# Summing the mLSTM half of y on GpSimd while heads are stored, in a decoder layer on one core

## The chip, the cores and the metric

One Trainium2 chip, one of its cores. The metric is the device time of one execution in microseconds (us). The engines go by the names of the profile: PE is TensorE, PEld its weight loads, DVE is VectorE, ACT is ScalarE, POOL is GpSimd, and SP is SyncE, which here only issues DMAs.

## The reference, cut to what matters

One layer of a decoder trunk, 1024 tokens, width 2048, all in float32:

```python
proj = x @ w_in                      # columns split over two head groups
# group A: sparse attention, 8 heads of 128 columns
score = sum_h w_i[h] * relu(q_i[h] @ k_i.T); sel = top_k(score, 256)
y_a = (softmax(q_lat @ c_sel.T + bias) @ c_sel @ w_uv) * silu(z_a)       # (1024, 1024)
# group B: mLSTM, 4 heads of 256 columns, chunkwise, then per-head norm
y_m = norm(h_m) * mh_norm_g * sigmoid(o_m) * silu(z_m)                   # (1024, 1024)
y = concat([y_a, y_m]) @ w_out
x = layer_norm(ALPHA * x + y)
```

## The kernel before

Work is laid out with 128 partitions (`P`), time in two halves `top` (tokens 0 to 511) and `bot` (512 to 1023). Every product that has to be exact to float32 is made of three passes over a rounded high part and a low rest: `split` casts on ACT (L106) and subtracts on DVE (L107). The order of instructions on each engine is set at compile time by a scheduler that follows priorities, edges written by hand (`issue_after`, `after`, `add_manual_dep`) and a model of time; at run time each engine takes its instructions in that order.

The stages, in order:

1. Projection of x for the indexer and search of the top 256 keys, then first halves of the other projections (to about 946 us).
2. The mLSTM stage: `Unit`s finish the other projections on PE (L679, 7 products of 12 matmuls each; sums of weights on POOL at L663, one low part on POOL at L668, accumulating weight DMAs on POOL at L644), and between them the four mLSTM heads run (`mlstm(h)`). Head h-1 is stored inside `mlstm(h)`, after the convolutions that give q and k: `stores(h-1)` calls `mlstm_store` for the two 128-column blocks j of the head, which transposes the head's output on PE, multiplies by the gate tile `sg` on DVE and writes `sg` (128 x 1024) to `y_d[8 + 2h + j]` in DRAM (L919). The last head is stored at the end of the stage.
3. Attention, 8 heads of 4 query blocks. `weights` adds the mask and bias tile on POOL (`nm`, L1249), reduces logits on DVE (L1256), and scales the exponentials by 1/sum on POOL (query tiles 4 to 7) or DVE (L1264). `turn` transposes them on PE (L1281), `mix` multiplies by the values (L1293 to L1296). A head's result goes to `y_d[h]`.
4. The output product with w_out, in blocks of Strassen-Winograd form: `Product(p, c)`, where p = 0 is the mLSTM half of y (`y_d[8..15]`) and p = 1 the attention half (`y_d[0..7]`). Each half has four blocks a11, a12, a21, a22 (columns j = 0 or 1, `top` or `bot`), each of 4 tiles of 128 x 512. The form also needs sums of these blocks, with signs already put in at storing: s1 = a21 + a22, s2 = s1 + a11, s4 = s2 + a12, s3 = a11 + a21.

The sums are prepared in DRAM while attention runs. `y_steps` names, by query block (4h + n), which steps are issued: a plain DMA on SP from DRAM to DRAM (L1154), or a DMA on POOL that adds to DRAM (`accum_op=OP.add`, L1151). Each step is two DMAs of 512 KB. So attention issues 10 copies on SP and 10 accumulating DMAs on POOL: s1, s2, s4 and s3 of p = 0, and s3 of p = 1. On POOL they stand between `nm` and the scaling of `weights`. `y_form` then loads the kept sums at the output (L1182). Sums that are not kept are loaded block by block (L1185) and added by POOL DMAs into SBUF (L1188).

SBUF working tiles of 128 x 1024 float32 come from one tag, `s4`, with 11 buffers; in the mLSTM stage q, k, the head's two outputs, `sg`, `ri`, `pq`, `kw`, `pqh`, `pql`, `kws`, `vraw`, `vh`, `vl` all live there. Raw weights have 6 buffers (`wraw`), split weights 4 pairs.

Of the kernel before, what the change touches and what calls it, by code (L numbers as in the profile page):

```python
# [15 lines left out]
OP = mybir.AluOpType  # L16
# [3 lines left out]
P = 128  # L20
# [46 lines left out]
SUMS = ("s1", "s2", "s3", "s4")  # L67
# [33 lines left out]
def kernel(ctx, tc, a, out):  # L101
    nc = tc.nc
    vec, act, pool, pe, sync = nc.vector, nc.scalar, nc.gpsimd, nc.tensor, nc.sync
# [36 lines left out]
    def small(j, p=P):  # L140
# [5 lines left out]
    y_d = dp.tile([KT, P, T], F32, name="y_d")  # L146
# [2 lines left out]
    part_d = dp.tile([NU, P, 2, T], F32, name="part_d")  # L149
    z_d = dp.tile([8, P, 2, 512], F32, name="z_d")  # L150
    y_form_d = {n: dp.tile([P, 4, 512], F32, name=f"y_form_d{n[0]}{n[1]}")
                for n in ((0, "s1"), (0, "s2"), (0, "s4"), (0, "s3"), (1, "s3"))}
    if_d = dp.tile([2 * H_M, T], F32, name="if_d")
    rows_d = dp.tile([H_M, 2, T], F32, name="rows_d")
    decay_d = dp.tile([H_M, NCH], F32, name="decay_d")
# [10 lines left out]
    def s4(name, shape=(P, T), dt=F32):  # L166
        return sp.tile(list(shape), dt, name=name, tag="s4", bufs=S4)
# [30 lines left out]
    def bank(name, shape=(P, 512)):  # L198
        return ss.tile(list(shape), F32, name=name, tag="b")
# [112 lines left out]
    n = len(marks)  # L312
# [261 lines left out]
    for i in range(2):  # L574
        ps = bank("vb")[0:H_A, 0:NV // 2]
        s = slice(i * NV // 2, (i + 1) * NV // 2)
# [23 lines left out]
    top, bot = halves  # L600
# [238 lines left out]
    for j in range(8):  # L839
        n = len(marks)  # L840
# [67 lines left out]
    def y_sign(left, upper):  # L908

        return -1.0 if left == upper else 1.0  # L910

    def mlstm_store(h, j, hs, sg):
        for half in range(2):
            ps = bank("ht")
            for c in range(4):
                pe.transpose(ps[:, c * P:(c + 1) * P], hs[half][:, c, j * P:(j + 1) * P], ident)
            vec.scalar_tensor_tensor(out=sg[:, halves[half]], in0=ps, scalar=y_sign(h < 2, half == 0),
                                     in1=sg[:, halves[half]], op0=OP.mult, op1=OP.mult)
        sync.dma_start(y_d[8 + 2 * h + j], sg)  # L919

    def mlstm_half(h, half, n, q, k):

        s = halves[half]
        ri = s4("ri", (P, 2, 512))
        sync.dma_start(ri, bcast_rows(rows_d[h, :, s]))
        pool.affine_select(out=ri[:, 0].rearrange("p (c l) -> p c l", l=L),
                           in_=ri[:, 0].rearrange("p (c l) -> p c l", l=L),
                           compare_op=OP.is_ge, fill=BIG, base=0,
                           pattern=[[0, 4], [1, L]], channel_multiplier=-1)
        pq = s4("pq", (P, 2, 512))  # L930
        for c in range(4):
            cs = slice(c * L, (c + 1) * L)
            act.activation(pq[:, 0, cs], ri[:, 0, cs], AF.Exp, scale=-1.0,
                           bias=gcol[:, half * 4 + c, 0, h:h + 1])
        with after(n):
            pt = bank("ktp")
            for c in range(4):
                cs = slice((half * 4 + c) * L, (half * 4 + c + 1) * L)
                pe.transpose(pt[:, c * P:(c + 1) * P], k[:, cs], ident)
            ps = bank("s")  # L940
            for c in range(4):
                cs = slice((half * 4 + c) * L, (half * 4 + c + 1) * L)
                pe.matmul(ps[:, c * L:(c + 1) * L], k[:, cs], q[:, cs], start=True, stop=True)
        kw = s4("kw", (P, 4, DK))
        vec.tensor_tensor(kw, pt.rearrange("p (c d) -> p c d", d=DK),
                          gcol[:, half * 4:half * 4 + 4, 1, h:h + 1].broadcast_to([P, 4, DK]),
                          op=OP.mult)
        vec.tensor_tensor(pq[:, 0], ps, pq[:, 0], op=OP.mult)
        vec.tensor_tensor(pq[:, 1], q[:, s], ri[:, 1], op=OP.mult)
        pqh, pql = s4("pqh", (P, 2, 512), F32R), s4("pql", (P, 2, 512), F32R)  # L950
        split(pqh, pql, pq)
        kws = s4("kws", (P, 2, 4, DK), F32R)
        split(kws[:, 0], kws[:, 1], kw)
        return pqh, pql, kws
# [139 lines left out]
    n = len(marks)  # L1094
# [14 lines left out]
    op = ctx.enter_context(tc.tile_pool(name="op", bufs=1))  # L1109
    Y = {}  # L1110

    def y_rows(p, name):

        j, s = {"a11": (0, top), "a12": (1, top), "a21": (0, bot), "a22": (1, bot)}[name]
        return [y_d[8 * (1 - p) + 4 * j + k][:, s] for k in range(4)]

    def y_tiles(pool_, name, tags=(None, None)):

        f = []
        for c, t in zip("hl", tags):  # L1120
            if pool_ is sp:
                y = [s4(f"y{name}{c}", (P, 2, 512), F32R) for _ in range(2)]
                f.append([y[k // 2][:, k % 2] for k in range(4)])
            else:
                y = pool_.tile([P, 4, 512], F32R, name=f"y{name}{c}", tag=t or f"y{name}{c}", bufs=1)
                f.append([y[:, k] for k in range(4)])
        return f
# [8 lines left out]

    chain, last_sum = [None], [None]

    def y_half(p, name, u):

        j, s = {"a11": (0, top), "a12": (1, top), "a21": (0, bot), "a22": (1, bot)}[name]
        k0 = 8 * (1 - p) + 4 * j + 2 * u
        return y_d[k0:k0 + 2, :, s].rearrange("k p c -> p k c")

    def y_step(p, name, src, more):

        for u in range(2):
            dst = y_form_d[p, name][:, 2 * u:2 * u + 2]
            if more:
                with tc.issue_after(last_sum[0].ins):  # L1150
                    pool.dma_start(dst, y_half(p, src, u), accum_op=OP.add)  # L1151
            else:
                src_ = y_form_d[p, src][:, 2 * u:2 * u + 2] if src in SUMS else y_half(p, src, u)
                d = sync.dma_start(dst, src_)  # L1154
                tc.add_manual_dep(d.ins, last_sum[0].ins.name, mybir.DependencyInfo(
                    mybir.DependencyClass.NoSync, mybir.DependencyReason.DATA), reason="pace")

    y_steps = {6: ((0, "s1", "a21", False), (0, "s3", "a11", False)),
# [4 lines left out]

    def y_form(p, name, pool_):

        early = p == 0 and name == "s1"
        kept = (p, name) in y_form_d
        if name in ("s2", "s4") and p:
            raw = chain[0]
        elif early:  # L1170
            raw = [s4("yraw", (P, 2, 512)) for _ in range(2)]
            raw = [raw[k // 2][:, k % 2] for k in range(4)]
        else:
            raw = oq.tile([P, 4, 512], F32, name="u" if name in ("s1", "s2", "s3") and (p == 0 or name == "s1") else "t")
            raw = [raw[:, k] for k in range(4)]
        if name == "s1":
            chain[0] = raw
        load, more = {"s1": ("a21", "a22"), "s2": (None, "a11"), "s4": (None, "a12")}.get(name, (name, None))
        f = y_tiles(sp if early else pool_, name)
        for k in range(4):  # L1180
            if kept:
                sync.dma_start(raw[k], y_form_d[p, name][:, k])  # L1182
            else:
                if load:
                    sync.dma_start(raw[k], y_rows(p, load)[k])  # L1185
                if more:
                    with tc.issue_after(last_sum[0].ins):
                        pool.dma_start(raw[k], y_rows(p, more)[k], accum_op=OP.add)  # L1188
            split(f[0][k], f[1][k], raw[k])
        return f  # L1190

    with ExitStack() as ph:
# [126 lines left out]
        for h in range(H_A):  # L1319
            qk = k_next + q_next  # L1320
            gt, tb = head_inputs(h) if h else head_0
            if h == 0:
                sync.dma_start(gt, gate_a[0])
            if h + 1 < H_A:
                k_next, q_next = keys(h + 1), queries(h + 1)
            order = range(4) if h < H_A - 1 else range(3, -1, -1)
            for n, p in enumerate(order):
                pr = weights(p, qk, tb)
                for step in y_steps.get(4 * h + n, ()):
                    y_step(*step)  # L1330
                consume(AHEAD - 1)
                if n == 0 and h % 2 == 0:
                    while blocks:
                        mix(blocks.pop(0))
                    values_of[h // 2] = values(h // 2)
                units.append((h, p, pr, gt, n == 3))
# [212 lines left out]
    for t in range(8):  # L1549
# [5 lines left out]
        for n in range(2):  # L1555
            ps = bank("zps") if t % 2 else lps()
            for kt in range(8):
                f = Y[("a11", "a12", "a21", "a22")[2 * i + kt // 4]]
# [57 lines left out]
```

## Time and profile before

| | |
|---|---|
| median of 3 runs | 1867.68 us (1867.62 to 1868.41) |
| profiled execution, own time | 1868.55 us |
| its span, first to last instruction | 1866.7 us |
| PE busy | 97% of the span |
| DVE, ACT, POOL busy | 71%, 50%, 20% |
| mean granted TensorE clock | 0.992 of full speed |

A row of a windows view gives the busy time of each engine inside a stretch: PE idle is the length of the stretch less PE busy. The granted clock is in its own column; at a clock below 1.00 the same matmuls take longer, so length x (1 - clock) is time lost too.

### The profile page before, as it was taken

Reading aid. Unit: us, or ns where it says so; the run is one execution under the profiler, and the core shown is the slowest. Engines: PE = TensorE matmul, PEld = TensorE weight load, DVE = VectorE, ACT = ScalarE, POOL = GpSimd, SP = SyncE. Lnnn points to the kernel's source line nnn. Section 1 sums busy time; section 2 is a strip of 40 time slices with the busy share of each in tenths; the row PEclk is TensorE's granted clock in tenths of the full one; section 3 lists DMA queues with packets and bytes.
Section 4 is the critical chain, followed back from the end, with each engine's and each line's share of the span. In section 5 each row is a group of like instructions: output and inputs, shape, how many; then the busy total and the mean of one; then the engine's idle time right before and its main releaser. Section 6 shows DMA issues by size and latency. Waiting matters only on the chain. (4 is left out here: it accounts for less than half of the span.)

```text
span 1866.7 us, 25500 instructions
## 1 busy us (share of the span) xinstructions
PE 1804.7 (97%) x8740; PEld 1518.4 (81%) x8740; DVE 1334.5 (71%) x2464; ACT 935.3 (50%) x1712; POOL 379.1 (20%) x368
## 2 busy tenths in 40 slices
PE   8999999999999999999999999989989999999997
PEld 7987888888877788788888787868878998788885
DVE  6264665887788778655667677777889876576788
ACT  5334444666658633432455565565655665343421
POOL 0021221011001000011322222222455541011132
PEclk9999999999999999999999999999999999999998
DMA  7355335346546557766565646556686437874764
GB/s 271 81 167 197 121 100 149 107 122 178 137 120 173 136 144 235 208 197 196 154 202 154 169 142 188 138 164 186 211 221 149 139 103 226 260 200 118 191 182 143
DMA packets 140699, 311.75 MB, mean 167 GB/s; under 512 B 14936, under 2 KB 25944, under 8 KB 134680
## 3 DMA queue, kind: packets, MB, share of 16 engines
q1 hardware_dynamic: 119416, 269.21, 44.4%
q0 software_dynamic: 21152, 40.90, 13.5%
q8 instruction: 69, 1.13, 0.3%
q14 instruction: 62, 0.51, 0.1%
HBM read 245.97 MB, written 77.72 MB: 173 GB/s over the span
## 5 line engine op out<-in xcount | busy, mean ns | idle before, releaser
L679 PE MATMUL pj<-xh,wh 128*128 128x512 f32 x912 | 360.0, 395 | 14.3 <-ACT wh L666 7.0
L679 PE MATMUL pj<-xh,wl 128*128 128x512 f32 x912 | 353.2, 392 | 5.2 <-DVE wl L670 5.2
L679 PE MATMUL pj<-xl,wh 128*128 128x512 f32 x912 | 357.3, 392 | 0.0
L666 ACT CAST wh<-wraw 128x512 fp32r<-128x512 f32 x266 | 163.0, 618 | 219.0 <-PE pj L679 100.9
L679 PEld LDWEIGHTS pj<-xh,wh 128*128 128x128 f32 x912 | 172.5, 189 | 53.9 <-ACT wh L666 10.3
L670 DVE TENSOR_TENSOR wl<-wraw,wh 128x512 fp32r<-128x512 f32 x247 | 171.8, 698 | 62.2 <-ACT wh L666 45.9
L679 PEld LDWEIGHTS pj<-xh,wl 128*128 128x128 f32 x912 | 172.0, 189 | 42.2 <-DVE wl L670 7.4
L679 PEld LDWEIGHTS pj<-xl,wh 128*128 128x128 f32 x912 | 172.6, 189 | 33.6
L644 POOL DMA_DIRECT2D wraw<-wg x76 | 66.3, 872 | 498.1 <-DMA wraw<-wg 249.3
L107 DVE TENSOR_TENSOR wl<-wraw,wh 128x512 fp32r<-128x512 f32 (+4 forms) x126 | 81.9, 655 | 95.5 <-ACT wh L106 81.8
L106 ACT CAST wh<-wraw 128x512 fp32r<-128x512 f32 (+4 forms) x126 | 70.4, 566 | 145.7 <-PE pj L216 57.6
L688 DVE TENSOR_TENSOR res<-res,pj 128x512 f32<-128x512 f32 x152 | 103.1, 680 | 38.9 <-PE pj L679 33.6
L473 DVE SCALAR_TENSOR_TENSOR sc<-r,wi,sc 128x384 f32<-128x384 f32 (+2 forms) x90 | 92.0, 1046 | 45.9 <-ACT r L468 45.3
L468 ACT ACTIVATE r<-sc 128x384 f32<-128x384 f32 (+3 forms) x160 | 79.5, 523 | 80.2 <-PE sc L467 73.8
L214 PE MATMUL pj<-xh,wh 128*128 128x512 f32 x320 | 103.7, 396 | 5.2 <-ACT xh L106 5.1
L216 PE MATMUL pj<-xl,wh 128*128 128x512 f32 x320 | 103.8, 394 | 0.0
L218 PE MATMUL pj<-xh,wl 128*128 128x512 f32 x320 | 103.0, 393 | 0.0
L594 POOL TENSOR_TENSOR wraw<-wraw 128x512 f32<-128x512 f32 x32 | 47.1, 1473 | 259.7 <-DVE st L321 110.7
L504 ACT ACTIVATE junk<-sc,cand 128x512 bf16<-128x512 f32 (+2 forms) x93 | 86.5, 931 | 5.9 <-DVE cand L519 5.7
L1249 POOL TENSOR_TENSOR nm<-mask,tb 128x256 f32<-128x256 bf16 (+3 forms) x64 | 67.5, 1142 | 87.2 <-DVE mn L1256 75.7
L663 POOL TENSOR_TENSOR wraw<-wraw 128x512 f32<-128x512 f32 x38 | 51.2, 1348 | 160.3 <-DVE wl L670 136.2
L507 DVE TENSOR_SCALAR_CACHE_REDUCE junk<-sc,cand 128x384 bf16<-128x384 f32 (+2 forms) x93 | 79.3, 875 | 0.7
(523 smaller groups left out, 4448.8 us busy)
## 6 DMA issues: line engine op xcount, KB each, us to landing
wraw<-wg SPq DMA_DIRECT2D x228, 256.0 KB, 4.2
wraw<-wg POOLq DMA_DIRECT2D x76, 256.0 KB, 5.8
part_d<-res SPq DMA_DIRECT2D x19, 1024.0 KB, 7.0
res<-part_d SPq DMA_DIRECT2D x18, 1024.0 KB, 7.9
wraw<-wo SPq DMA_DIRECT2D x64, 256.0 KB, 4.9
wraw<-wv SPq DMA_DIRECT2D x48, 256.0 KB, 5.2
wraw<-xT SPq DMA_DIRECT2D x32, 256.0 KB, 2.9
z<-x SPq DMA_DIRECT2D x16, 512.0 KB, 6.4
```

What stands on the lines that cost most here:

```text
L107: vec.tensor_tensor(lo, src, hi.bitcast(F32), op=OP.subtract)
L214: pe.matmul(ps[i], wh, xh(k, i), start=k == k_first, stop=False)
L216: pe.matmul(ps[i], wh, xl(k, i), start=False, stop=False)
L218: last_mm[0] = pe.matmul(ps[i], wl, xh(k, i), start=False, stop=k == k_last)
L468: act.activation(r[:, s], ps, AF.Relu)
L473: vec.scalar_tensor_tensor(out=sc[t], in0=r, scalar=wcol, in1=sc[t], op0=OP.mult, op1=OP.add)
L504: act.activation(junk, sc[t], AF.Sign, scale=-1.0, bias=th[:, t - 2:t - 1], accum_out=cnt[:, t - 2:t - 1])
L507: vec.tensor_scalar(junk, sc[t], th[:, t - 2:t - 1], 0.0, op0=OP.is_lt, op1=OP.add, accum_out=cnt[:, t - 2:t - 1])
L666: last_cast[0] = act.copy(wh, src)
L670: last_low[0] = vec.tensor_tensor(wl, src, wh.bitcast(F32), op=OP.subtract)
L679: last_mm[0] = pe.matmul(ps, w[:, k], x[:, k], start=start and k == 0 and n == 0, stop=k == 3 and n == 2, skip_group_check=True)
L688: vec.tensor_tensor(dst, dst, ps, op=OP.subtract if minus else OP.add)
```

## The change

- For heads 0 and 1, after `sg` is stored, POOL adds its `top` and `bot` halves in SBUF into a new `s4` tile `f` and SP stores the result as block 2h + j of the kept s3: 4 adds and 4 stores of 256 KB.
- For head 2, head 0's block is loaded from `y_d[8 + j]` into `f` (512 KB), and POOL makes s1, s2 and s4 from it and `sg`, each stored by SP: 2 loads, 6 adds, 6 stores of 256 KB, two `s4` tiles (`f`, `f4`) for each j.
- Only the tiles of heads 1 and 3 (tiles 2 and 3 of each block) are still summed in DRAM during attention, for s1, s2 and s4: one DMA of 512 KB for each step, 3 copies on SP and 3 accumulating DMAs on POOL.
- s3 of the attention half (p = 1) is no longer kept: `y_form` loads a11 and adds a21 by a POOL DMA for each of its 4 tiles, at the output.

```diff
@@ mlstm_store, after sync.dma_start(y_d[8 + 2 * h + j], sg)
+        if h < 2:
+            f = s4("f", (P, 512))
+            pool.tensor_tensor(f, sg[:, top], sg[:, bot], op=OP.add)
+            sync.dma_start(y_form_d[0, "s3"][:, 2 * h + j], f)
+        elif h == 2:
+            f, f4 = s4("f"), s4("f4", (P, 512))
+            sync.dma_start(f, y_d[8 + j])
+            for name, out, x, y in (("s1", f[:, bot], f[:, bot], sg[:, bot]), ("s2", f[:, top], f[:, top], f[:, bot]),
+                                    ("s4", f4, f[:, top], sg[:, top])):
+                pool.tensor_tensor(out, x, y, op=OP.add)
+                sync.dma_start(y_form_d[0, name][:, j], out)
@@ attention
-    y_steps = {6: ((0, "s1", "a21", False), (0, "s3", "a11", False)),
-               8: ((0, "s1", "a22", True), (0, "s3", "a21", True)),
-               11: ((0, "s2", "s1", False),), 13: ((0, "s2", "a11", True),),
-               16: ((0, "s4", "s2", False),), 18: ((0, "s4", "a12", True),),
-               20: ((1, "s3", "a11", False),), 22: ((1, "s3", "a21", True),)}
+    def y_last(name):
+        j, s = {"a11": (0, top), "a12": (1, top), "a21": (0, bot), "a22": (1, bot)}[name]
+        return y_d[10 + 4 * j:12 + 4 * j, :, s].rearrange("k p c -> p k c")
+    def y_step(name, src, more):
+        dst = y_form_d[0, name][:, 2:]
+        src = y_form_d[0, src][:, 2:] if src in SUMS else y_last(src)
+        if more:
+            with tc.issue_after(last_sum[0].ins):
+                pool.dma_start(dst, src, accum_op=OP.add)
+        else:
+            d = sync.dma_start(dst, src)
...
+    y_steps = {6: ("s1", "a21", False), 8: ("s1", "a22", True), 11: ("s2", "s1", False),
+               13: ("s2", "a11", True), 16: ("s4", "s2", False), 18: ("s4", "a12", True)}
@@ y_form
-        load, more = {"s1": ("a21", "a22"), "s2": (None, "a11"), "s4": (None, "a12")}.get(name, (name, None))
+        load, more = {"s1": ("a21", "a22"), "s2": (None, "a11"), "s4": (None, "a12"), "s3": ("a11", "a21")}.get(name, (name, None))
```

## Rows read from the trace of the kernel before

**Rows 1.** Windows by stage: stretch, length, PE, PEld, DVE, ACT, POOL busy, clock, DMA.

```profile
946.00:1320.00 374.00, 358.10 (x1728) 296.93 (x1727) 274.78 (x510) 217.08 (x355) 97.59 (x84) 0.99 0.57 163
1320.00:1546.00 226.00, 212.05 (x1422) 193.28 (x1422) 194.08 (x474) 138.15 (x286) 110.03 (x118) 0.98 0.59 166
1546.00:1866.70 320.70, 305.07 (x1337) 250.03 (x1335) 235.31 (x384) 110.89 (x193) 51.49 (x48) 0.98 0.67 190
```

**Rows 2.** Windows of attention, one for each head from the third on.

```profile
1362.00:1394.00 32.00, 25.29 (x162) 22.43 (x161) 30.05 (x66) 18.87 (x40) 18.75 (x18) 0.95 0.84 203
1394.00:1422.00 28.00, 25.91 (x189) 24.17 (x188) 24.15 (x57) 16.11 (x35) 12.50 (x15) 1.00 0.61 158
1422.00:1446.00 24.00, 22.07 (x143) 20.55 (x142) 22.29 (x55) 13.70 (x30) 13.17 (x15) 0.93 0.64 157
1446.00:1474.00 28.00, 26.90 (x198) 25.20 (x197) 22.77 (x58) 16.27 (x34) 13.18 (x15) 1.00 0.61 161
1474.00:1495.00 21.00, 21.00 (x149) 19.63 (x148) 20.86 (x56) 14.31 (x31) 11.71 (x13) 1.00 0.28 94
1495.00:1520.00 25.00, 24.36 (x176) 22.57 (x176) 21.00 (x57) 17.77 (x34) 13.34 (x14) 1.00 0.30 107
1520.00:1546.00 26.00, 26.00 (x171) 23.60 (x170) 15.64 (x37) 12.91 (x29) 7.02 (x8) 1.00 0.47 108
```

**Rows 3.** Line L1151: duration in ns (min/median/max), first and last start in us.

```profile
L1151 POOL DMA_DIRECT2D y_form_d0s<-y_d x8: 1127/1600/2556, 1367.3 to 1433.6; - x8
L1151 POOL DMA_DIRECT2D y_form_d1s<-y_d x2: 1097/1326/1554, 1463.6 to 1464.3; - x2
```

**Rows 4.** DVE timeline (start, us, instruction) in two heads; then line L1264 on DVE.

```profile
1371.81 4.28 DVE L107 TENSOR_TENSOR ql<-qraw,qh 128x1024 fp32r<-128x1024 f32 x1 [0.15 <-ACT qh L106]
1478.77 1.22 DVE L107 TENSOR_TENSOR ql<-qraw,qh 128x1024 fp32r<-128x1024 f32 x1
L1264 DVE TENSOR_SCALAR lg<-lg,sm x32: 347/526/3229, 1339.3 to 1531.7; 128x256 f32<-128x256 f32 x16, 128x384 f32<-128x384 f32 x8, 128x512 f32<-128x512 f32 x8
```

**Rows 5.** PE timeline, third attention head; in brackets the idle time before and its end.

```profile
1379.49 0.69 PE L110 MATMUL lps<-kh,qh 128*128 128x384 f32 x1 [4.33 <-DVE mn L1256]
```

**Rows 6.** POOL's additions by line, mLSTM stage: busy us, mean ns, idle before.

```profile
L663 POOL TENSOR_TENSOR wraw<-wraw 128x512 f32<-128x512 f32 x32 | 42.3, 1323 | 123.5 <-DVE wl L670 99.4 <-DVE vv L1038 8.3 <-DMA wraw<-wg 6.7
L668 POOL TENSOR_TENSOR wl<-wraw,wh 128x512 fp32r<-128x512 f32 x16 | 25.3, 1584 | 4.4 <-ACT wh L666 4.4
```

**Rows 7.** DVE and POOL timelines of the mLSTM stage, just after head 0 is stored.

```profile
1020.88 1.27 DVE L884 SCALAR_TENSOR_TENSOR q<-res,smalls,q 128x1022 f32<-128x1022 f32 x1
1022.07 2.32 DVE L884 SCALAR_TENSOR_TENSOR k<-res,smalls,k 128x1022 f32<-128x1022 f32 x1
1020.91 2.39 POOL L668 TENSOR_TENSOR wl<-wraw,wh 128x512 fp32r<-128x512 f32 x1
```

**Rows 8.** Windows of the mLSTM stage that follow the stores of heads 0, 1, 2.

```profile
1044.00:1062.00 18.00, 15.25 (x65) 12.36 (x64) 10.13 (x16) 7.34 (x16) 3.66 (x4) 0.91 0.72 199
1117.00:1160.00 43.00, 39.00 (x185) 31.34 (x185) 32.02 (x45) 23.64 (x37) 11.86 (x10) 1.00 0.65 195
1228.00:1262.00 34.00, 29.59 (x135) 23.34 (x134) 20.95 (x30) 21.54 (x33) 8.99 (x9) 0.91 0.58 165
```

**Rows 9.** SP timeline: head 2's stores; then a DMA group, median us to landing.

```profile
1232.00 0.92 SPq L919 DMA_DIRECT2D y_d<-sg  x2
y_d<-sg SPq DMA_DIRECT2D x8, 512.0 KB, 3.9
```

**Rows 10.** Output stage, tile t and line L1188: ns (min/median/max), start us; L1188's landing.

```profile
L1182 SPq DMA_DIRECT2D t<-y_form_d1s x4: 319/403/425, 1641.0 to 1642.3; - x4
L106 ACT CAST ys3h<-t x4: 613/616/618, 1678.4 to 1679.9; 128x512 fp32r<-128x512 f32 x4
L1188 POOL DMA_DIRECT2D u<-y_d x4: 859/859/1144, 1659.2 to 1664.0; - x4
DMA to landing us min/median/max: 3.9/6.2/7.6
```

More of the change, by code (lines that the diff above doesn't have):

```diff
@@ L151 @@
     y_form_d = {n: dp.tile([P, 4, 512], F32, name=f"y_form_d{n[0]}{n[1]}")
-                for n in ((0, "s1"), (0, "s2"), (0, "s4"), (0, "s3"), (1, "s3"))}
+                for n in ((0, "s1"), (0, "s2"), (0, "s4"), (0, "s3"))}
     if_d = dp.tile([2 * H_M, T], F32, name="if_d")
@@ L1137 @@
     chain, last_sum = [None], [None]
-    def y_half(p, name, u):
+    def y_last(name):
         j, s = {"a11": (0, top), "a12": (1, top), "a21": (0, bot), "a22": (1, bot)}[name]
[L1142 to L1156, printed above, removed]
-    y_steps = {6: ((0, "s1", "a21", False), (0, "s3", "a11", False)),
[4 rows of a table removed]
+        return y_d[10 + 4 * j:12 + 4 * j, :, s].rearrange("k p c -> p k c")
[7 more added lines that the diff above has]
+            d = sync.dma_start(dst, src)
+            tc.add_manual_dep(d.ins, last_sum[0].ins.name, mybir.DependencyInfo(
+                mybir.DependencyClass.NoSync, mybir.DependencyReason.DATA), reason="pace")
+    y_steps = {6: ("s1", "a21", False), 8: ("s1", "a22", True), 11: ("s2", "s1", False),
+               13: ("s2", "a11", True), 16: ("s4", "s2", False), 18: ("s4", "a12", True)}
     def y_form(p, name, pool_):
@@ L1328 @@
                 pr = weights(p, qk, tb)
-                for step in y_steps.get(4 * h + n, ()):
-                    y_step(*step)
+                if 4 * h + n in y_steps:
+                    y_step(*y_steps[4 * h + n])
                 consume(AHEAD - 1)
```

## The prediction

> **What bounds the kernel now.** PE is busy for 97% of the span (the table above), so the kernel is bound by PE, and only PE idle time and time at a lowered clock can be won. I read the windows by stage first, for the three stages that the change touches [rows 1]: PE idle, length less busy, is 15.9 us in the mLSTM stage, 14.0 in attention and 15.6 in the output.
>
> Next the same view by attention head [rows 2]. The four heads from 1362 to 1474 us leave PE idle for 6.71, 2.09, 1.93 and 1.10 us, 11.83 in all; the three heads after 1474 leave 0.00, 0.64 and 0.00. The heads do the same kind of work. What differs is the accumulating DMAs that POOL issues: the line's rows [rows 3] put all ten between 1367 and 1464 us (four in the first of these heads, two in each other). So the idle time goes with them. Where the clock falls below 1.00 it costs more: 0.05 x 32 = 1.60 us in the first of these heads and 0.07 x 24 = 1.68 us in the third, 3.28 together [rows 2].
>
> How a DMA on POOL can stop PE is seen in the DVE timeline [rows 4]. The same subtraction `ql` takes 4.28 us just after the four DMAs were issued and 1.22 us in a head without them; the scaling of L1264 runs from 347 to 3229 ns. I read this so: POOL, held up by issuing, then runs its late `nm` and scaling instructions in a row, and DVE is kept waiting beside them. The logits behind on DVE come late, and PE stands for 4.33 us [rows 5]. That DVE is the link is plain from its busy time, 30.05 of 32 us in that head [rows 2].
>
> **The change part by part: attention.** Ten POOL issues become three (query blocks 8, 13, 18), of 512 KB each as before. The price of one issue, from the four heads, is 11.83 / 10 = 1.18 us of idle PE and 3.28 / 10 = 0.33 of clock, 1.51 together [rows 2, 3]. Seven go: 7 x 1.51 = 10.6 us won. The most it can be is all of it, 15.1. The least: the three remaining steps each cost what a pair costs now, and the fourth step goes. Then 2.09 + 2.09 + 1.93 = 6.1 of the 11.83 stays, 5.7 is won, and nothing from the clock. I take the middle, since the rows show stalls that grow with the number of issues in a row (6.71 for four, 1.1 to 2.1 for two), so that one should cost about one.
>
> The ten copies on SP become three. SP computes nothing, and PE does not wait for them; I cost this at nothing and count no gain, though the DMA share of 0.84 in the first of these heads [rows 2] should fall.
>
> **The change part by part: mLSTM stage.** Added on POOL are 4 adds for heads 0 and 1 and 6 for head 2, all of 128 x 512. The nearest row is the weight sum of the same size, 1323 ns [rows 6]: 10 x 1.32 = 13.2 us of POOL, which is busy only 97.6 of 374 us there [rows 1]. What could make them cost PE time is what they delay: POOL's next weight sum (L663) and low part (L668), and DVE instructions that run at the same moment. One such meeting stands in the trace: beside a POOL subtraction of 2.39 us a convolution step of DVE took 2.32 us instead of 1.27, so 1.05 more [rows 7]. The adds fall just there, because heads are stored right after, or during, the convolutions of the next head.
>
> Bounds for the cost: nothing, if all hides behind the other POOL idle time; 13.2 us, if each add holds up PE for its own length. The stage has 48 such POOL instructions (32 + 16, [rows 6]) and 15.9 us of PE idle altogether [rows 1], so even if all that idle time came from them one costs 0.33 us. I take 10 x 0.33 = 3.3 us; it is nearer to the lower end because POOL is idle three quarters of the stage.
>
> The Trainium skill bears on this ("SBUF — State Buffer", section "Who interferes with whom"): DVE and GpSimd share a port pair, held for a whole instruction, and a DVE instruction with two SBUF inputs waits for a GpSimd one that reads SBUF. The meeting in [rows 7] agrees with it. By that rule alone, with every add in the way of DVE, this part would cost its upper bound and not 3.3; the last rival says what the time would then be.
>
> The loads and stores that come with the adds (2 of 512 KB, 10 of 256 KB) stand on SP's queue before weight loads. A store waits for its add, so at worst each weight load behind it waits 1.3 us; the stores of `sg` land in 3.9 us [rows 9], and six `wraw` buffers lie between a load and PE. I cost the queue at nothing on that cover; without it, 12 issues of 0.33 us are 4 us, inside the bound above.
>
> **Buffers.** `f` takes an `s4` buffer until its store lands: one add and 3.9 us, some 5 us, for two tiles at heads 0 and 1. By the code 8 of the 11 are then live (q, k, two `sg`, `ri`, `pq`, and shortly the old outputs), so two more fit. At head 2, `f` and `f4` of both j take four buffers from the load on, for a load, three adds in a row and a store: 4 + 3 x 1.3 + 4, some 12 us, from 1232 [rows 9] to about 1244. There they just fit or just don't; that is the second rival.
>
> **The change part by part: output.** `t` for s3 of the attention half is now loaded as before, but from a11, and then gets an accumulating DMA for each of its 4 tiles. It was issued from 1641.0 to 1642.3 us and read by ACT only at 1678.4 [rows 10]. Four POOL issues of 0.86 us and a landing of 6.2 come to 9.6 us, and POOL works little in this stage (51.5 of 320.7 us, [rows 1]). The cover is about 32 us, so I cost it at nothing; without the cover it would be 9.6.
>
> **Sum.** -10.6 + 3.3 = -7.3 us against the profiled execution's own 1868.55 us (its span plus 1.85 around it, which I leave as it is) gives 1861.2. That execution is 0.9 above the median of the runs, 1867.68; I say 1861.
>
> **Rivals.**
>
> *The gain is small* (no change). The remaining three issues cost what pairs cost now: -5.7 + 3.3 = -2.4, 1866.1. For it: DVE is nearly full in those heads anyway (30.05 of 32, 22.29 of 24 [rows 2]), and one late POOL instruction can start a row of collisions. Against it: two of the three later heads run with no PE idle and a DVE nearly as full (20.86 of 21).
>
> *Buffers of `s4` run out at the head boundaries* (slower). The windows after the stores of heads 0, 1 and 2 are where the mLSTM stage stands still already: 2.75 + 4.00 + 4.41 = 11.2 us of idle PE, and 0.09 x 18 + 0.09 x 34 = 4.7 at a lowered clock [rows 8]. If `f` delays `ri`, `pq` or `vraw` of the next head and this doubles, it costs 15.9: -10.6 + 15.9 = +5.3, 1873.8. It decides from the point where the mLSTM part costs more than the 10.6 won. For it: the place is the same, and the buffer count at head 2. Against it: at heads 0 and 1 the tiles are free again some ten microseconds before the second half of the head fills all 11.
>
> *All ten issues' cost goes* (faster by more): -15.1 + 3.3 = -11.8, 1856.7. For it: one issue alone may find POOL with slack and start no row of collisions.
>
> *Every add holds up DVE and PE for its length*: -10.6 + 13.2 = +2.6, 1871.2. For it: [rows 7], where both were lengthened. Against it: 48 such instructions now cost at most 15.9 us, not 48 x 1.4.
> This is the case in which the port rule cited above, from the Trainium skill, decides alone.
>
> A change of under 0.2% (3.7 us) is what a measurement of this kernel can't tell from none.
>
> **How the numbers follow.** My forecast 0.54, all gone 0.08: faster 0.62. Small gain 0.14, every add in the way (within 0.2%) 0.06: same 0.20. Buffers run out: slower 0.18. The bounds on the terms alone reach from 1868.55 - 15.1 = 1853.4 to 1868.55 - 5.7 + 13.2 = 1876; the range leaves out the low edge and most of the buffer case above its milder half: 1854 to 1872. The likeliest case's own range is 1857 to 1864.
>
> **What would show it.** Right: in attention three POOL issues of `y_step`; no `ql` or L1264 over 2 us except next to them; PE idle in the heads from the third on some 3 to 4 us instead of 11.8; clock 1.00 there. In the mLSTM stage PE idle 16 to 20 us. In the output `ys3h` not waiting for `t`. Wrong: DVE instructions of 3 to 4 us in attention that stay without an issue beside them; PE idle after 1232 us that grows by more than 5; a `vraw` or `ri` issued later than now against PE's place; or SP waiting for `f` with weight loads behind it.

## The result, and the profile after

The changed kernel takes 1876.62 us (median of 6 runs, 1872.59 to 1880.09) against 1867.83 for the kernel before, timed beside it: ratio 1.0054, 95% interval 1.0037 to 1.0071. It is slower, by half a per cent and clear of the noise; forecast were 1861 us and a gain of 7.

The page of the changed kernel, its first part (busy us, share, instructions), and its windows by the stages of [rows 1]:

```profile
PE 1808.5 (96%) x8740; PEld 1519.8 (81%) x8740; DVE 1333.3 (71%) x2464; ACT 934.2 (50%) x1711; POOL 385.6 (21%) x375
```

```profile
946.00:1320.00 374.00, 355.91 (x1701) 295.59 (x1700) 273.64 (x492) 208.92 (x342) 109.15 (x94) 0.98 0.59 172
1320.00:1546.00 226.00, 214.04 (x1445) 195.09 (x1444) 193.56 (x492) 143.88 (x296) 100.98 (x111) 0.99 0.45 134
```

TensorE's idle time grew from 15.9 to 18.1 us in mLSTM and shrank from 14.0 to 12.0 in attention; the granted clock in mLSTM is 0.98 and was 0.99, which over 374 us is up to 4 us more. Fixed windows shift against work that runs late, so the rest of this text uses a ledger. Both programs have 8740 matmuls; the lag is the start of the n-th matmul in one trace less its start in the trace of before, each counted from its program's first matmul, read where before stands at the given time. (The compile-time scheduler changes the order in places, so it is the n-th matmul and not always the same one; where the order changes, at 1320 and 1362 above all, a mark read some us earlier or later moves by 1 to 4 us.)

```
us into before's span     960   1200   1320   1362   1474   1546   1650   1700   1850
lag of the new kernel    -1.6    2.4    6.8    8.3   -0.2   -0.3    2.3    8.2    8.3
```

From 960 to 1362 us, mLSTM and the first attention heads, 9.9 us are lost; in the heads from 1362 to 1474, 8.5 are won; in the output, behind 1546, 8.6 are lost. With -1.6 from before the change and -0.1 that makes +8.3, and the profiled runs are 1876.79 - 1868.55 = 8.24 apart. Of three terms one came about nearly as forecast, and two cost some 15 us more.

**mLSTM, heads 0 and 1.** Timelines of POOL, DVE and PE in the changed kernel, where head 0 has just been stored (start, duration, instruction, idle time before it and what ended it):

```profile
1017.33 2.83 POOL L922 TENSOR_TENSOR f<-sg 128x512 f32<-128x512 f32 x2
1019.98 1.42 POOL L668 TENSOR_TENSOR wl<-wraw,wh 128x512 fp32r<-128x512 f32 x1
```

```profile
1017.54 4.96 DVE L884 SCALAR_TENSOR_TENSOR k<-res,smalls,k 128x1023 f32<-128x1023 f32 x1
1022.42 0.67 DVE L688 TENSOR_TENSOR res<-res,pb 128x512 f32<-128x512 f32 x1
```

```profile
1026.13 0.50 PE L679 MATMUL pj<-xh,wh 128*128 128x512 f32 x1 [3.30 <-DVE res L688]
```

The two new adds and the low part behind them run back to back until 1021.4. The convolution step, 1.27 us alone [rows 7], takes 4.96 and ends 1.1 us after the last of the three; PE waits 3.30 us for what DVE does behind it. The two adds of head 1 hold a step of DVE almost as long:

```profile
1124.36 3.66 DVE L884 SCALAR_TENSOR_TENSOR q<-res,smalls,q 128x1021 f32<-128x1021 f32 x1
```

Yet the lag grows by 4.2 us from 1020 to 1028 us, and by only 1.0 from 1100 to 1200, where e14 below, which has no adds, falls back by as much (1.3). Before has 4.00 us of idle PE behind head 1's store already [rows 8], the changed kernel 2.96 in the same window.

**mLSTM, head 2.** SP's timeline, then one line each of POOL and DVE, then PE's:

```profile
1199.00 0.42 SPq L926 DMA_DIRECT2D f<-y_d  x1
...
1233.44 0.92 SPq L919 DMA_DIRECT2D y_d<-sg  x2
...
1239.13 0.41 SPq L930 DMA_DIRECT2D y_form_d0s<-f  x1
1239.63 0.38 SPq L926 DMA_DIRECT2D f<-y_d  x1
1240.11 0.44 SPq L930 DMA_DIRECT2D y_form_d0s<-f  x1
1242.37 0.33 SPq L641 DMA_DIRECT2D wraw<-wg  x1
1247.94 2.02 SPq L930 DMA_DIRECT2D y_form_d0s<-f  x2
1250.06 0.39 SPq L936 DMA_DIRECT2D ri<-rows_d  x1
...
1268.58 0.54 SPq L969 DMA_DIRECT2D vraw<-v_d  x1
```

```profile
1246.63 1.28 POOL L929 TENSOR_TENSOR f<-f,sg 128x512 f32<-128x512 f32 x1 [2.85 <-DMA f<-y_d]
```

```profile
1255.33 0.69 DVE L960 TENSOR_TENSOR pq<-q,ri 128x512 f32<-128x512 f32 x1 [6.86 <-DMA ri<-rows_d]
```

```profile
1257.36 0.77 PE L679 MATMUL pb<-xh,wh 128*128 128x512 f32 x1 [5.45 <-DVE kw L956]
1257.93 0.63 PE L679 MATMUL pb<-xl,wh 128*128 128x512 f32 x1
```

The same two loads in before:

```profile
1234.41 1.70 SPq L925 DMA_DIRECT2D ri<-rows_d  x1
...
1252.23 0.53 SPq L958 DMA_DIRECT2D vraw<-v_d  x1
```

In before `ri` of the last head is issued 2.4 us after the store of [rows 9] and `vraw` 20.2 us after it; here 16.6 and 35.1. `ri` stands behind stores that wait for adds, and those adds wait for the second `f` load, which is issued just behind a store at 1239.63 and read at 1246.63. DVE then stands 6.86 us for `ri`; `kw`, which does not need `ri`, is behind that step in DVE's order, and PE waits 5.45 us for `kw`. Behind that wait matmuls of 0.39 us take 0.63 for some 5 us: the granted clock is 0.50 from 1258 to 1262 us, its level of 1.2 GHz, and it is 0.50 there in before too. By 1310 us the lag has grown by only 1.5 us from 1200, and by 4.4 more at 1362: the rest comes where the last head's results are due, with waits of PE of 0.87 us for `rd` and 1.22 for `num`.

**Attention.** Three accumulates of 1.1 to 1.2 us are left, none in a row with another. Their line in the changed kernel (ns min/median/max, first and last start), then the window of the four heads that [rows 2] gives one by one:

```profile
L1161 POOL DMA_DIRECT2D y_form_d0s<-y_d x3: 1114/1139/1203, 1380.5 to 1436.3; - x3
```

```profile
1362.00:1474.00 112.00, 105.60 (x738) 97.98 (x737) 100.26 (x251) 68.08 (x143) 48.96 (x52) 0.98 0.45 126
```

PE idle is 6.4 us there, in place of 11.8.

**Output.** POOL's timeline, then SP's, DVE's and PE's, in the changed kernel:

```profile
1647.42 2.63 POOL L1194 DMA_DIRECT2D t<-y_d  x3 [55.65 <-DVE wl L1362]
1651.76 0.86 POOL L1194 DMA_DIRECT2D t<-y_d  x1 [1.71 <-DMA t<-y_d]
1662.44 1.75 POOL L1381 DMA_DIRECT2D t_sum<-wo  x2 [9.82 <-DMA t_sum<-wo]
```

```profile
1647.91 2.38 SPq L1379 DMA_DIRECT2D t_sum<-wo  x2
```

```profile
1663.03 0.69 DVE L1400 TENSOR_TENSOR wraw<-wraw 128x512 f32<-128x512 f32 x1 [4.80 <-DMA wraw<-wo]
```

```profile
1671.37 0.50 PE L1423 MATMUL lps<-wl,ys3h 128*128 128x512 f32 x1 [1.44 <-DVE wl L107]
1680.66 0.50 PE L1423 MATMUL lps<-wl,ys3h 128*128 128x512 f32 x1 [0.58 <-DVE wl L107]
1685.56 0.76 PE L1423 MATMUL lps<-wh,ya22h 128*128 128x512 f32 x1 [2.34 <-DVE z L1455]
```

The lines of `t_sum` in before:

```profile
1645.58 1.66 SPq L1373 DMA_DIRECT2D t_sum<-wo  x2
```

```profile
1654.00 1.75 POOL L1375 DMA_DIRECT2D t_sum<-wo  x2 [64.91 <-PE lps L1417]
```

The new accumulates into `t` themselves are early enough. But the loads issued beside them come late. That of `t_sum`, issued 2.3 us later than before, is ready for its own accumulate 14.5 us after its issue, not 8.4, so that runs 8.4 us later. And DVE waits 4.80 us for a load of raw weights (`wraw`), a wait that before and e1 below do not have and e4 has (4.7 us). PE waits for weights `wl` and for `z`, which DVE makes behind these; which of the two late loads sets them isn't told apart. From 1650 to 1700 us PE is busy 45.63 of 50 us at a clock of 0.97; in before it is 49.18 at 1.00. In the changed kernel:

```profile
1650.00:1700.00 50.00, 45.63 (x191) 36.39 (x191) 32.51 (x53) 18.19 (x32) 8.79 (x11) 0.97 0.87 220
```

### The profile page after: what moved, and what is told of

The parts are those of the page before. It is cut to its first block, busy times and chain, and to the rows that moved or that the text cites. A ratio compares the mean times of both kernels' runs of the same rounds, so it can differ in the third digit from the quotient of the medians.

```text
span 1875.0 us, 25518 instructions
## 1 busy us (share of the span) xinstructions
PE 1808.5 (96%) x8740; PEld 1519.8 (81%) x8740; DVE 1333.3 (71%) x2464; ACT 934.2 (50%) x1711; POOL 385.6 (21%) x375
## 3 DMA queue, kind: packets, MB, share of 16 engines
q0 software_dynamic: 19824, 38.28, 12.4%
## 4 chain that ended last, share of the span: by engine, by line
PE 71%; DMA 12%; DVE 11%; issue 3%; ACT 3%; SPq 1%; POOL 0%; DVEq 0%; ACTq 0%; POOLq 0%
PE pj L679 24%; PE pb L679 4%; PE lps L1423 4%; PE pj L214 4%; PE pj L218 4%; PE pj L216 4%; PE pj L787 3%; DMA wraw<-wo 3%; PE pc L787 2%; PE sc L466 2%; PE sc L467 2%; DMA wraw<-wg 1%; PE pb L1423 1%; PE lps L110 1%; PE lps L111 1%
## 5 line engine op out<-in xcount | busy, mean ns | idle before, releaser
L1255 POOL TENSOR_TENSOR nm<-mask,tb 128x256 f32<-128x256 bf16 (+3 forms) x64 | 62.6, 1023 | 89.3 <-DVE mn L1262 74.6
```

## The experiments

In the experiments the kernel before was timed anew beside each group: medians of 1866.2 to 1867.5, with single runs spread over some 10 us. A ledger is one run; among kernels whose first 960 us are the same the lag there differs by up to 4 us, so only differences between columns are read, and small ones not at all. The profiled runs of e6, e12 and e13 are the fastest or nearly the fastest of their kernels. The ledgers of all but e8, as above:

```
kernel                    960   1200   1320   1362   1474   1546   1650   1700   1850
e1_s3_kept               -3.9    1.3    6.8    8.0   -1.5   -1.5    0.4    0.5    0.2
e4_s3_at_output_alone    -3.7   -2.5   -3.9   -3.9   -2.7   -2.7   -0.9    4.2    3.6
e2_dve_adds              -2.4    6.1   11.5   17.0    8.6    8.4   10.4   16.2   15.2
e3_both                  -2.3    6.3   12.2   18.7    8.3    8.2    9.9    9.8    9.2
e5_heads01               -2.9    1.2   -0.3   -0.0   -1.9   -2.0   -1.1   -1.3   -1.1
e6_head2                 -3.6   -3.1   -0.1    0.6   -5.7   -5.7   -5.8   -5.3   -6.2
e7_no_adds               -3.7   -2.4    4.2   10.0   -0.7   -0.7    1.1    0.7   -0.3
e11_order_kept           -2.2   -0.1    6.1    8.6    0.5    0.6    2.5    2.4    2.4
e12_order_alone          -2.2   -3.1   -1.5   -1.8   -3.2   -3.2   -3.1   -3.6   -3.2
e10_dram_in_mlstm        -1.2    0.0    0.5    7.1   -0.8   -0.8    0.6    0.9   -0.0
e13_less_s4              -2.8   -3.2   -5.2   -3.1  -10.2  -10.3   -8.6   -8.5   -8.9
e14_neither              -4.0   -3.0   -4.9   -2.7  -10.3  -10.3   -8.9   -8.7   -9.4
e15_pool_queue           -3.8   -2.0   11.9   16.2    9.0    8.9   10.7   10.7    9.8
e16_after_ri             -2.2    1.7   16.9   18.8    9.6    9.6   11.1   11.2   10.3
```

**Output: is it the moved s3?** e1 puts the second form's s3 back into attention; e4 moves it alone.

```diff
 e1 = changed kernel
+    y_other(...)   # (1, "s3") copied and accumulated in DRAM at blocks 20 and 22, as before
 e4 = kernel before
-    20: ((1, "s3", "a11", False),), 22: ((1, "s3", "a21", True),)
+    load, more = {..., "s3": ("a11", "a21")}   # as in the changed kernel
```

> The changed kernel, but s3 of the attention half is again summed in DRAM during attention (two copies, two accumulating DMAs) and only loaded at the output. Theory A: the 8 us that the output lost come from forming s3 there, whose accumulating DMAs make the later POOL DMAs late; so 1876.6 less about 7, plus about 1 for the two POOL issues: 1869 to 1871. Rival B: the output's loss is DMA timing that any shift would bring; then 1875 to 1878.

> The kernel before with one part of the change alone: s3 of the attention half is no longer summed during attention but loaded and added at the output. Theory A: output +6 to +8, attention -1 to -1.5 for the two POOL issues fewer: 1872 to 1875. Rival B: 1866 to 1868.

Measured: e1 1869.08 (ratio 1.0009, 0.9994 to 1.0024), e4 1873.41 (1.0033, 1.0012 to 1.0054). The step between 1546 and 1850, +8.6 in the changed kernel, is +1.7 in e1 and +6.3 in e4. Both times lie where theory A had them. Shown: computing s3 at the output costs 6 us by itself and some 7 on the changed kernel; the 1.7 that e1 keeps have another cause, which isn't known. Leaving the two steps in attention costs nothing there: e1 wins 9.5 us between 1362 and 1474, the changed kernel 8.5, and e4, without the two, wins nothing.

**Are the adds' collisions with DVE the mLSTM loss?** e2 and e3 run the ten adds on VectorE.

```diff
 e2 = changed kernel, e3 = e1
-            pool.tensor_tensor(f, sg[:, top], sg[:, bot], op=OP.add)
+            vec.tensor_tensor(f, sg[:, top], sg[:, bot], op=OP.add)
-                pool.tensor_tensor(out, x, y, op=OP.add)
+                vec.tensor_tensor(out, x, y, op=OP.add)
```

> The changed kernel with its ten block sums in the mLSTM stage on VectorE instead of GpSimd. Theory A: the mLSTM stage lost about 8 us because the adds run in a row on POOL, hold up DVE's convolutions and stand before POOL's weight sums; on DVE an add should take 0.7 us, and the loss falls to 2 to 4: 1869 to 1872. Rival C: the s4 buffers that f and f4 hold are the cause; then the time stays at 1874 to 1878.

> Both edits at once: s3 of the attention half kept in DRAM as before, the ten adds on VectorE. Theory A with both parts right: 1862 to 1865, faster than both kernels, since the attention gain of about 7 is left. With B and C both true: 1874 or more. One of the two true: 1868 to 1871.

Measured: e2 1884.07 (1.0102, 1.0070 to 1.0134), e3 1879.33 (1.0066, 1.0046 to 1.0086). Theory A's forecasts missed both times. e2 lies above both of its ranges; e3 lies where B and C together would have it, but e1 and e4 had ruled B out. DVE and PE of e3 where head 0 is stored:

```profile
1019.12 1.27 DVE L884 SCALAR_TENSOR_TENSOR k<-res,smalls,k 128x1023 f32<-128x1023 f32 x1
```

```profile
1022.84 0.50 PE L679 MATMUL pj<-xh,wh 128*128 128x512 f32 x1 [0.73 <-DVE res L688]
...
1062.18 0.58 PE L110 MATMUL num<-vh,pqh 128*128 128x258 f32 x1 [6.82 <-ACT vh L106]
```

The stall at 1020 is gone (1.27 us in place of 4.96, a wait of 0.73 in place of 3.30), so it was POOL's run. But 40 us later PE waits 6.82 us for `vh`: `vraw` is issued at 1051.64, in before at 1047.80. So the adds cost PE more on DVE than on POOL (8.6 us from 960 to 1200, e1 5.2), by another chain, read from the rows and not tested by itself: `ri`, `pq`, the buffers they free, `vraw`, `num`.

**Which heads?** e5 keeps only the four sums of heads 0 and 1, e6 only the six of head 2; the others are made in DRAM during attention.

```diff
 e5 = e1
-        elif h == 2: ...              # s1, s2, s4: all four tiles in attention
 e6 = e1
-        if h < 2: ...                 # (0, "s3"): in attention
```

> Of the ten sums on GpSimd only the four of heads 0 and 1 (s3 of the first form) are kept; s1, s2 and s4 are made in DRAM during attention for all four tiles, as in before, and the second form's s3 too, so that attention issues two accumulates less than before. Theory A (each sum costs where it is run, because GpSimd's run of adds holds VectorE's convolution and a weight chain waits for it): the steps at the stores of heads 0 and 1 stay (about +5 us by 1155 against before), the +4 to +5 between 1245 and 1310 go; attention gives back 2 to 4; time 1867 to 1870. Theory B (head 2's buffers are the whole loss): no loss in mLSTM, time 1863 to 1866.

> Of the ten sums on GpSimd only the six of head 2 are kept; the s3 of both forms is made in DRAM during attention, as in before. Theory A (each sum costs where it is run): no step at 1020 and 1125 against before, +4 to +6 between 1245 and 1310; attention gives back 3 to 5 us of its accumulates; time 1866 to 1869. Theory B (head 2's buffers are the whole loss): the whole +8 at 1320 is left, time 1870 to 1873.

Measured: e5 1868.48 (1.0008, 0.9993 to 1.0024), e6 1865.03 (0.9990, 0.9975 to 1.0004). As theory A has it each group costs where it stands: e5 loses 4.1 us by 1200 and gives 1.2 back by 1362, e6 loses nothing by 1200 and 3.7 after it. In time e5 is inside theory A's range and e6 1 us below it.

**The adds, or the stores with them?** e7 leaves the ten additions and the two `f` loads out and stores halves of y unsummed, so its output is not the reference's.

```diff
 e7 = e1
-            f = s4("f", (P, 512))
-            pool.tensor_tensor(f, sg[:, top], sg[:, bot], op=OP.add)
-            sync.dma_start(y_form_d[0, "s3"][:, 2 * h + j], f)
+            sync.dma_start(y_form_d[0, "s3"][:, 2 * h + j], sg[:, bot])
...
+            for name, s in (("s1", bot), ("s2", top), ("s4", top)):
+                sync.dma_start(y_form_d[0, name][:, j], sg[:, s])
```

> The ten sums of mLSTM's heads and their tiles and two loads are left out; the stores go out as they are, of halves of y itself, so the output is not the reference's. Second form's s3 in DRAM during attention as in before. Theory A (the sums and their buffers cost the 8 us in mLSTM, attention gives back about 9): mLSTM at before's pace, time 1858 to 1862. Rival (the eight more stores on SyncE's queue cost them): mLSTM still 5 to 8 us behind before by 1320, time 1866 to 1869.

Measured: 1870.02 (1.0009, 0.9992 to 1.0026). The step of head 0 is gone (-3.7 to -2.4 by 1200), but head 2's is 12.4 us from 1200 to 1362. At heads 0 and 1 the price is the adds with their `f` tiles, and not the stores; at head 2 stores, with the order that the scheduler then gives, are enough for a loss. This was the rival, with a time 1 us above its range, and not what I believed.

**Is it the order?** The scheduler puts the `num` products of the last head later in all kernels with head 2's sums or stores. e11 is e1 with before's order of PE, DVE and ACT from head 2's store to attention; e12 is before with e1's order there, and nothing else.

```diff
 e11 = e1, e12 = kernel before
+    for x, y in zip(seq, seq[1:]):    # the other kernel's order, without a wait
+        tc.add_manual_dep(y, x.name, NoSync)
```

> e1_s3_kept with all ten sums on GpSimd, but TensorE, VectorE and ScalarE issue their instructions from head 2's store to the first attention head in the order of the kernel before (edges without a wait; the compile-time scheduler had put head 3's products of num and up some 40 matmuls later because of the sums). Theory O (head 2's loss of 4 to 8 us between 1245 and 1350 is the changed order): the lag against before stays near +2 at 1350 in place of +8, time 1861 to 1865. Theory S (the loss is the sums themselves: GpSimd's run, their buffers, SyncE's queue): the order of before waits on late data as much or more, lag at 1350 of +6 to +10 and time 1867 to 1872.

> The kernel before with nothing changed but the order of TensorE, VectorE and ScalarE between head 2's store and the first attention head: it is the order of e1_s3_kept. Theory O (the changed order is the loss): +4 to +6 us between 1245 and 1350, time 1871 to 1874. Theory S (the sums are the loss): before's time within 2 us, 1866 to 1870.

Measured: e11 1871.88 (1.0028, 1.0016 to 1.0041), e12 1871.88 (1.0027, 1.0010 to 1.0043). Before's order doesn't save e11: 8.7 us from 1200 to 1362. The order alone costs e12 5 us in the median, as theory O had it, but the profiled run of e12 is among its fastest (1865.26 of 1865.11 to 1877.68) and loses 1.3 from 1200 to 1362; where most of these 5 us lie isn't seen. Two waits are. PE of e12:

```profile
1314.88 0.47 PE L686 MATMUL pj<-xh,wh 128*128 128x512 f32 x1 [0.87 <-DVE rd L1046]
1319.10 0.88 PE L925 MATMUL ht<-ident,num 128*128 128x128 f32 x6 [1.22 <-ACT num L1054]
```

These are the waits of the changed kernel at 1323 and 1327 us, of the same length, in a kernel without a sum; e1 and e6 have them too, before, e11 and e14 do not. So they belong to the order. The wait for `kw` does not: e12 has none, and e11, in before's order, has one of 8.27 us where e1 has 5.72.

**Neither sums nor stores.** In e14 they are left out and the parts of `y_form_d` are filled far earlier with other data, so its output is not the reference's. The order of mLSTM is before's.

```diff
 e14 = e1
-        if h < 2: ...
-        elif h == 2: ...
+        if i in (5, 6, 7, 9):   # in the first half's units
+            d = sync.dma_start(y_form_d[0, n_][:, w], form_d[0, "s1"][:, w])
```

> e1_s3_kept without the sums at the heads' stores and without their eight stores and two loads; the parts of y_form_d that they wrote are filled some 500 us earlier by four copies of other data, so the output is not the reference's. Attention has e1_s3_kept's short list of steps, mLSTM has the kernel before's order of instructions. Theory S (sums and stores at the heads' boundaries cost about 8 us, and five accumulates in place of ten give 8 to 9 back in attention): lag near 0 at 1350, attention -7 to -10, time 1857 to 1861. Rival (attention only regains a delay that it was handed; from an undelayed start it gives 2 or less): time 1864 to 1868.

Measured: 1857.09 (0.9953, 0.9939 to 0.9967), as theory S. mLSTM costs 1.3 us in its ledger and attention gives 7.6 from an undelayed start, so the gain there is no regained delay. Each against the before beside it, e1 is 1.5 us above and e14 9.1 below, 10.7 apart: that is the price of ten adds with their stores and loads and the order that comes of them, at places where the next head's inputs are issued. SP of e14 behind the store of head 2:

```profile
1230.51 0.93 SPq L925 DMA_DIRECT2D y_d<-sg  x2
1232.15 0.33 SPq L641 DMA_DIRECT2D wraw<-wg  x1
1232.58 1.36 SPq L931 DMA_DIRECT2D ri<-rows_d  x1
...
1248.91 0.54 SPq L964 DMA_DIRECT2D vraw<-v_d  x1
```

**The sums in DRAM, but earlier.** e10 makes them by copies and accumulates one at a time from head 2's last unit on; e13 leaves s4 in attention.

```diff
 e10 = e1 without its sums
+    plan = {2: [[("s3", False)]], 3: [[("s3", True), ("s1", False)], [("s1", True)],
+            [("s2", False)], [("s2", True)], [("s4", False)], [("s4", True)]]}
 e13 = e10
-            [("s4", False)], [("s4", True)]
+    if 4 * h + n in (16, 18): in_dram("s4", 4 * h + n == 18, last_sum)
```

> No sum on an engine and no buffer: the first form's s3 and heads 0 to 2's share of s1, s2 and s4 are made in DRAM as in before, by plain copies of SyncE and accumulates of GpSimd's queue, but one after another during mLSTM's last head and the two units behind it, not during attention; second form's s3 in DRAM during attention. Theory S (the sums on engines at the heads' stores cost the 8 us in mLSTM, fewer issues in attention give 8 to 9 back): mLSTM within 3 us of before, time 1858 to 1863. Rival (any work added to mLSTM's last head costs there what attention gives back): +5 or more by 1350, time 1866 to 1870.

> e10_dram_in_mlstm, but the first two tiles of s4 are copied and accumulated in attention, at the slots of the rest of s4, so that no transfer of a sum is under way when the first query is loaded at 1324. Theory Q (e10's step of 4.6 us at 1320 is the query's load behind and beside those two transfers): no step there, attention -6 to -8, time 1859 to 1863. Rival (the sums' transfers cost wherever mLSTM's last head takes them): time 1865 to 1868.

Measured: e10 1865.81 (1.0002, 0.9987 to 1.0017), e13 1864.60 (0.9992, 0.9982 to 1.0002). e10 lies between its two forecasts. It stands level with before until 1320 (+0.5) and is 7.1 behind at 1362. ACT and PE there:

```profile
1336.91 1.04 ACT L106 CAST qh<-qraw 128x1024 fp32r<-128x1024 f32 x1 [4.85 <-DMA qraw<-qa_d]
```

```profile
1338.01 0.39 PE L110 MATMUL lps<-kh,qh 128*128 128x256 f32 x1 [3.74 <-ACT qh L106]
```

The first query, issued at 1324.3, is loaded beside s4's copy and accumulate (issued 1318.3 and 1323.5) and read 12.6 us after its issue; in before ACT reads it after 6.6. Without them the step is gone in e13's profiled run (-3.1 at 1362), and the run took 1859.56; but that is the fastest of 11, and the median of 1864.60 is no gain that can be told from none. So theory Q is shown for the step, in one run of e13, and missed for the time.

**Queue or buffers at head 2?** e15 issues the sums' loads and stores on POOL's queue; e16 writes head 2's sums behind the `ri` loads, so that the gated tile keeps its buffer longer.

```diff
 e15 = e1
-            sync.dma_start(y_form_d[0, "s3"][:, 2 * h + j], f)     # and the other nine
+            pool.dma_start(y_form_d[0, "s3"][:, 2 * h + j], f)
 e16 = e1
             parts = [mlstm_half(h, half, ...) for half in range(2)]
+            while late:
+                late_sums(*late.pop(0))    # head 2's f, f4, adds, stores
```

> e1_s3_kept with the sums' eight stores and two loads issued by GpSimd's queue in place of SyncE's; the sums are as before. Theory Q (head 2's loss is SyncE's queue: the next head's ri load stands behind stores that wait for adds): ri is issued by 1237 in place of 1249, TensorE's wait of 5.7 us for kw at 1256 goes, head 2's step against e14_neither falls from 8 to 3 or less, time 1861 to 1866. Rival (GpSimd's own time is the price, and ten more issues there add to it): head 2's step stays at 8 or grows, time 1869 to 1874.

> e1_s3_kept with head 2's two loads, six sums and six stores written behind the two ri loads of the last head, so that SyncE issues ri first; the gated output tile stays in its buffer until then. Theory Q: the wait of 5.7 us for kw at 1256 goes, time 1862 to 1867. Rival (the sums' buffers are the price wherever they stand): vraw is issued at 1265 or later and num is as late as in e1_s3_kept, time 1868 to 1873.

Measured: e15 1878.09 (1.0069, 1.0051 to 1.0087), e16 1878.17 (1.0065, 1.0046 to 1.0084): the rivals' side both times, and 4 to 5 us above the rivals' ranges. SP of e16, then PE:

```profile
1233.72 0.92 SPq L919 DMA_DIRECT2D y_d<-sg  x2
1236.20 1.63 SPq L941 DMA_DIRECT2D ri<-rows_d  x1
...
1259.34 0.33 SPq L931 DMA_DIRECT2D f<-y_d  x1
...
1282.24 0.54 SPq L974 DMA_DIRECT2D vraw<-v_d  x1
```

```profile
1288.32 0.58 PE L110 MATMUL num<-vh,pqh 128*128 128x258 f32 x1 [10.21 <-ACT vh L106]
```

`ri` is early, as wanted, and PE's wait for `kw` is gone, as theory Q had it; so that wait came from the sums ahead of `ri`. But `vraw` comes 48.5 us after the store, and PE waits 10.21 us for `vh`, which is made from it. The waits on SP's queue from 1225 to 1290 us (us in total, times, longest) name `pql`, a tile of the `s4` buffers, for the `f` load before it, so a sum here does wait for a buffer:

```profile
SPq L931 <- DVE pql L107: 11.0, 1, 11.0
```

e15 moved the wait and did not take it away. `ri` is issued 9.4 us after the store, but POOL stands 6.67 us for the second `f` load, so that its next sum of weights runs at 1252.32; ACT waits 9.20 us for that sum, DVE 5.85 for ACT, `kw` is behind this in DVE's order, and PE waits 10.34 us for `kw`. So e15 shows that POOL's queue is no better a place, and not that SP's costs nothing.

Across the kernels, us from head 2's store to the issue of the last head's first `vraw`, beside the growth of the lag from 1200 to 1362:

```
                e14   before  e13   e5    e10   e7    e11   e3    e2    e12   after  e1    e6    e15   e16
vraw            18.4  20.2    21.0  19.9  20.9  27.2  29.1  30.1  30.2  30.5  35.1   35.5  34.2  41.1  48.5
lag, 1200-1362   0.3   0.0     0.1  -1.2   7.1  12.4   8.7  12.4  10.9   1.3   5.9    6.7   3.7  18.2  17.1
```

Where `vraw` is on time nothing is lost (e10's 7.1 is the query's step above); where it is late 4 to 18 us are, but for e12, whose order takes `num` later and which has no sums. How late it is does not say how much is lost (27.2 and 12.4 in e7, 34.2 and 3.7 in e6). It is late in each way of placing the sums beside the head's own tiles in the 11 `s4` buffers. A twelfth buffer, which would tell buffers from the rest, wasn't tried. (e8, with `f` in the raw weights' buffers, was forecast at 1867 to 1870 or 1861 to 1865 us and took 1907.31: it loses 22 us by 1200 and 29 more by 1362, so these buffers were not free either.)

## Why the prediction was wrong

*What bounds the kernel* held: what moved the time is PE's idle time, and in mLSTM a lower clock beside it.

*Attention, -10.6 forecast, -8.5 in the ledger.* The mechanism and nearly the price were right. By 1.51 us an issue, five issues fewer should win 7.6; the eight kernels of the ledger with five fewer (e1, e3, e7, e10, e11, e14, e15, e16) win 7.2 to 10.7, so that e14 has just 7.6 is luck. The last two issues, those of the second form's s3, gave nothing back, here and in e4: that is the 2 us too many. The marks that I named hold in part. There are three issues, and the long scalings (L1270) stand behind them, but each of the three still has one: 3.28, 2.78 and 3.08 us, within 5 us of its issue. PE idle is 6.4 us in place of 11.8, where I had 3 to 4, and the clock 0.98 and not 1.00.

*Output, 0 forecast, +8.6 measured.* This step failed: "The cover is about 32 us, so I cost it at nothing." The cover was counted to the reader of `t` alone. The work that was due next was other: `t_sum`, on the same queue of POOL, and the raw weights `wraw`, both being loaded at that moment. I had the price without the cover, 9.6, and set it aside. e1 and e4 show that some 7 of the 8.6 are the moved s3; that the four accumulates lengthen the landing of `t_sum` and `wraw` is read from the rows and not tested by itself.

*mLSTM, +3.3 forecast, +9.9 measured, inside the bounds 0 to 13.2.* The term of 0.33 us an add was the step that failed first: it shared out the idle time of before over all POOL instructions. At heads 0 and 1 the link is the one that I named, POOL's run in DVE's way, and larger, 3.7 us on one convolution step at head 0; at head 1 it is 2.4 on another, which costs PE hardly anything, since in before it stands there anyway. The port rule of the Trainium skill ("SBUF — State Buffer", "Who interferes with whom") agrees with the place: the step reads two SBUF inputs and stands still beside POOL's adds. By that rule for every add the part would be 13.2; the ledger has 9.9, and 5.9 of it stand behind 1200 us, where e7 loses more without an add. There, at head 2, the step that failed is "I cost the queue at nothing on that cover": six buffers of raw weights don't cover `ri` and `vraw`, which stand on the same queue and need `s4` buffers. The paragraph on buffers failed too: I had `f` and `f4` from 1232 us to 1244, but the first `f` load is issued at 1199.00, and its tile is held until the store at 1239.13 lands, over 40 us. My sign of a failure there, `ri` or `vraw` issued later with SP waiting for `f`, is what came.

*The rivals.* "Buffers run out" named the place and gave 1873.8, which is nearer to 1876.6 than any other; but that is luck, since it had the gain of attention whole and no loss at the output. Without the output's loss the changed kernel would take the time of e1, 1869.1, so mLSTM by itself ate the gain, and the output made the change slower. That s3 at the output could cost was no rival of mine.

*What stays open.* How all of head 2's loss divides between buffers, stores on SP's queue and the scheduler's order. The wait for `kw` comes of `ri` behind the sums (e12 and e16 don't have it), the two waits at the last head's end are the order (e12 has them). But e7 shows that the adds aren't needed for a loss, e11 that before's order doesn't cure it, e12 that the other order costs 5 us in time by itself, and e16 that an earlier `ri` doesn't cure it, since `vraw` is then later.

## What to carry to other kernels

A cover is counted for everything that stands next on the queue and in the buffers that the moved work uses, not only for the one who reads its result. Work added at a boundary where the next stage's inputs are issued is priced by those inputs' lateness: the ten adds are 14.7 us on an engine that is idle three quarters of the time, and with their loads and stores cost some 11 us on TensorE's path (e1 less e14). Before a gain is looked for by moving work, a kernel that leaves the work out shows what there is to win at most; here it was 9 us, and no placement that was tried kept more than 2 of them, none of them clear of the noise. A delay is priced where it falls: a DVE step held by POOL's adds cost PE 4 us at head 0 and next to nothing at head 1, where PE stood already.

## What the runs showed of the hardware

A DVE instruction with two SBUF inputs waited through three POOL instructions in a row, 3.7 us, and not just for one (4.96 us in place of 1.27, at 1017.54), and another through two (3.66, at 1124.36); with the adds on DVE the first took 1.27 (e3). A plain load of 256 KB beside accumulating transfers was ready for its reader after 14.5 us where it had been after 8.4 (`t_sum`). One of 512 KB was read 12.6 us after its issue where it had been read after 6.6 (`qraw`, e10).
